# A hybrid decoder layer on one core: three 256-column matmuls per weight tile into one set of PSUM columns

## The chip, the cores and the metric

The kernel runs as one program on one core of a Trainium2 chip. The metric is the device time of one execution in microseconds (us): the kernel before takes 2576.43 us, the median of three runs (2575.58 to 2576.53). A profile of one execution tells what each engine did in it: TensorE (PE in the rows, its weight loads PEld), VectorE (DVE), ScalarE (ACT), GpSimd (POOL) and the queues of DMA (SP issues most of them).

## The reference

One layer of a decoder trunk, 256 tokens of 2048 features, everything float32:

```
h = RMSNorm(x); P = h @ W_in               (mLSTM: 4 heads x 256; dilated attention: 8 heads x 128)
x += concat(mLSTM, dilated attention) @ W_out
x += CrossAttention(RMSNorm(x), RMSNorm(mem))        (4 heads of 512, 256 memory tokens; W_xq, W_xk, W_xv, W_xo)
x += PEER(RMSNorm(x))
out = RMSNorm(x)
```

PEER has 16384 experts of one neuron each: `q = h @ W_pq`, for each of 8 heads the best 16 of 128 keys of both halves, from them the best 16 pairs, a softmax over these, and `sum over experts of gate * gelu(u_e . h) * v_e`. The kernel computes `gelu(u_e . h)` of all 16384 experts, multiplies by a gate that is zero for those not picked, and multiplies by the whole table `v`. So nearly all the work is in matrix products that are streamed once from HBM: tiles of 128 partitions x 2048 float32 (1 MB each).

## The kernel before, in words

Features or experts lie on partitions and the 256 tokens in the free dimension. Each operand of a large product is split into two parts of type `float32r`, hi and lo, whose sum is the float32 value. ScalarE casts a half of a weight tile (128 x 1024) to hi (line 111), and VectorE or GpSimd subtracts to get lo (line 112). GpSimd does it in part of the first stage and for the experts' tiles while VectorE picks the experts. The moving operand (the activations) lies in a buffer of 16 chunks of 512 columns: columns 0 to 255 the hi part of 256 tokens, columns 256 to 511 their lo part.

A product keeps three of the four partial products: hi x hi, hi x lo and lo x hi. For a tile of weights `lin_a` goes over 16 chunks of the contraction. For each it issues two matmuls: hi weights times 512 columns (line 126), which writes hi x hi to PSUM columns 0 to 255 and hi x lo to columns 256 to 511; and lo weights times the first 256 columns (line 127), which adds to columns 256 to 511. The experts' second table has the same pair of matmuls in `v_tile` (lines 818 and 819), the gates of the mLSTM heads in lines 242 and 243. After the last chunk the two halves of the PSUM tile are added: ScalarE copies one half out, VectorE adds the other (`join` at line 253, `join_scaled` at 523, `residual_block` at 185 to 188, `u_block` at 629 and 630, the queries of the experts at 691 and 692), or VectorE adds both to the residual (lines 823 and 824). The other kind of product, `lin_b` (lines 138 to 140), has the activations as weights and 512 columns of weights as the moving operand; it issues three matmuls of 512 columns into the same PSUM columns.

Every matmul has a weight load of its own in the trace (13610 of each), also where it has the same weights as the one before it, as in lines 138 and 139.

The program runs in this order. From 0 to about 330 us the projections of both groups of heads, with the small work of the heads in generators that go one step on after each tile of weights. From about 330 us to 870 us `W_out`, the keys, queries and values of the cross attention, and `W_xo`. From 870 us to 1070 us the product with `W_pq` and the picking of experts, mostly on VectorE, with some blocks of the table `u` (`u_block`) between. From 1070 us to 1290 us the remaining blocks of the first 32, and between them the gates, which are spread into a dense table by one-hot products (`gate_group`, lines 748, 749 and 755). From 1290 us to 2540 us the table `v` (128 tiles, `v_tile`) with the remaining 96 blocks of `u` between. A scheduler puts the instructions of each engine in order when the program is built; on the chip each engine goes through its own in that order, and waits for the others by semaphores. The loads of weights have three buffers (line 97), hi and lo three each.

Of the kernel before, what the change touches and what calls it, by code (L numbers as in the profile page):

```python
# [10 lines left out]
F32 = mybir.dt.float32  # L11
# [9 lines left out]
P = 128  # L21
# [27 lines left out]
def hybrid_layer(ctx: ExitStack, tc: tile.TileContext, a, out):  # L49
# [53 lines left out]
    def wsplit(st, lo_engine=None, order=(0, 1)):  # L103
        """the parts of the tile's two halves; lo_engine "both" gives the half used last to GpSimd"""
# [16 lines left out]

    def lin_a(ps, hi, lo, mov, kcs=range(KC)):
        """ps[:, :256] + ps[:, 256:] = W.T @ h; mov(k) holds both parts of h's chunk."""
        kcs = list(kcs)
        for n, k in enumerate(kcs):
            PE.matmul(ps, hi(k * P), mov(k), start=(n == 0), stop=False)  # L126
            PE.matmul(ps[:, 256:], lo(k * P), mov(k)[:, :256], start=False,  # L127
                      stop=(n == len(kcs) - 1))

    def lin_b(pss2, kg, hi, lo, h):  # L130
        """pss2[tt] += h[:, tt].T @ W for four chunks of the contraction."""
# [10 lines left out]
    def rstd_of(dst, ss, n):  # L142
        """dst = (ss / n + eps) ** -0.5: a first guess from the exponent's bits, three steps of Newton's method"""
# [28 lines left out]
    def as_column(row, name):  # L172
        """[P, 256] with equal partitions -> [P, 2], tokens on partitions."""
# [8 lines left out]
    def residual_block(pool, ps, n, g_at, acc, nxt, first):  # L182
        """resid += ps; acc += resid ** 2; nxt = both parts of resid * g"""
        tmp = pool.tile([P, T], F32, tag="rtmp", name=f"rtmp{n_mm[0]}", bufs=2)
        S.copy(tmp, ps[:, 256:])
        x = resid[:, n, :]
        V.tensor_tensor(x, x, ps[:, :256], op=OP.add)
        V.tensor_tensor(x, x, tmp, op=OP.add)
# [32 lines left out]
    with tc.tile_pool(name="ph1", bufs=2) as p1:  # L221
# [9 lines left out]
        hm = lambda k: h[:, k, :]  # noqa: E731  # L231
        ps_g = mm_tile()
        parts = []
        for i in range(4):
# [5 lines left out]
            for k in range(4 * i, 4 * i + 4):  # L240
                c = (k - 4 * i) * P
                PE.matmul(ps_g, hi[:, c:c + P], hm(k), start=(k == 0), stop=False)
                PE.matmul(ps_g[:, 256:], lo[:, c:c + P], hm(k)[:, :256], start=False, stop=(k == KC - 1))
# [5 lines left out]
        def join(dst, ps, tag):  # L249
            """dst = ps[:, :256] + ps[:, 256:]"""  # L250
            tmp = p1.tile([P, T], F32, tag="jtmp", name=f"jtmp{n_mm[0]}_{tag}")
            S.copy(tmp, ps[:, 256:])
            V.tensor_tensor(dst, ps[:, :256], tmp, op=OP.add)

        def head_norm(sq_parts, n, name):
            """rstd over the head's features, on every partition"""
# [9 lines left out]
        def proj_rows(src, dst):  # L266
            """one group of 512 columns, tokens on partitions: dst [P, 2, 512]"""
# [15 lines left out]
        def start_chain():  # L283
# [8 lines left out]
            for dst, r0, b_at in ((gi, 0, S_BI), (gf, 32, S_BF)):  # L292
                S.copy(gt, ps_g[r0:r0 + 4, 256:])
                S.copy(gu, ps_g[r0:r0 + 4, :256])
                V.tensor_tensor(dst, gu, gt, op=OP.add)
# [85 lines left out]
        rows, ogs = {}, {}  # L381

        def mlstm_in(hd):
            """causal conv on the head's two blocks of channels"""
# [4 lines left out]
            for j in range(2):  # L389
                blk = 2 * hd + j  # L390
                ps = mm_tile()
# [3 lines left out]
                join(xin[:, 3:], ps, f"in{blk}")  # L395
                V.tensor_tensor(xin[:, 3:], xin[:, 3:], rx, op=OP.mult)
# [9 lines left out]
        def mlstm_chain(hd, c32, wq):  # L406
# [4 lines left out]
            # decay weights exp(a_s - max_t), keys on partitions  # L411
# [10 lines left out]
            # q, k: [features, tokens]  # L422
# [23 lines left out]
            # denominator, on every partition  # L446
# [29 lines left out]
        def output_gate(hd):  # L476
            og = p1.tile([P, 2, T], F32, tag="og", name=f"og_{hd}")
            for j in range(2):
                ps = mm_tile()
                lin_a(ps, *wtile(a["w_mo"][2 * hd + j], "both"), hm)  # L480
                join(og[:, j, :], ps, f"o{hd}{j}")
                V.tensor_tensor(og[:, j, :], og[:, j, :], stat["row"], op=OP.mult)
# [15 lines left out]
    # ================= cross attention =================  # L498
    with tc.tile_pool(name="ph2", bufs=1) as p2:
# [18 lines left out]
        mm_ = lambda k: mh[:, k, :]  # noqa: E731  # L518

        def join_scaled(dst, ps, r):  # L520
            tmp = p2.tile([P, T], F32, tag="jt", name=f"jt{n_mm[0]}", bufs=2)
            S.copy(tmp, ps[:, 256:])
            V.tensor_tensor(dst, ps[:, :256], tmp, op=OP.add)
            if r is not None:
                V.tensor_tensor(dst, dst, r, op=OP.mult)
# [435 lines left out]
```

## Time and profile before

| | |
|---|---|
| median of three runs | 2576.43 us |
| span of the profiled execution, first to last instruction | 2554.4 us |
| what lies around the span (median less span) | 22.0 us |
| TensorE busy | 2436.9 us, 95% of the span, 13610 matmuls and as many weight loads |
| VectorE busy | 1724.6 us, 68% |
| ScalarE busy | 1202.1 us, 47% |
| GpSimd busy | 401.6 us, 16% |
| DMA | 466.78 MB, 183 GB/s |

A page of the profile gives the busy time of each engine and its share of the span. TensorE's matmuls are pipelined and their ends are modelled, so rows of neighbouring matmuls overlap, and the pace is read from the distance between two starts. A row "x2048 | 734.2, 400" is a group of 2048 instructions with 734.2 us of busy time and 400 ns mean duration. Where a timeline row has "x2", it merges two neighbours of one line. The profiled execution's time outside its span is not in the profile; the three runs lie within 1 us of each other, so the table takes the difference to their median.

### The profile page before, as it was taken

Reading aid. Unit: us, or ns where it says so; the run is one execution under the profiler, and the core shown is the slowest. Engines: PE = TensorE matmul, PEld = TensorE weight load, DVE = VectorE, ACT = ScalarE, POOL = GpSimd, SP = SyncE. Lnnn points to the kernel's source line nnn. Section 1 sums busy time; section 2 is a strip of 40 time slices with the busy share of each in tenths; the row PEclk is TensorE's granted clock in tenths of the full one; section 3 lists DMA queues with packets and bytes.
Section 4 is the critical chain, followed back from the end, with each engine's and each line's share of the span. In section 5 each row is a group of like instructions: output and inputs, shape, how many; then the busy total and the mean of one; then the engine's idle time right before and its main releaser. Section 6 shows DMA issues by size and latency. Waiting matters only on the chain.

```text
span 2554.4 us, 34778 instructions
## 1 busy us (share of the span) xinstructions
PE 2436.9 (95%) x13610; PEld 2117.2 (83%) x13610; DVE 1724.6 (68%) x2818; ACT 1202.1 (47%) x1649; POOL 401.6 (16%) x214
## 2 busy tenths in 40 slices
PE   7989999999999879788899999999999999999997
PEld 6777788888888768677888888888888888888886
DVE  6877758744456699899975555655655655556565
ACT  6555446444445434355554444444444444444343
POOL 3131313100001457545400000000000000000001
PEclk9999999999999989899999999999999999999998
DMA  6344435544544434344485656555655565555553
GB/s 244 140 144 148 139 125 205 191 168 173 175 176 169 166 119 162 128 167 184 183 289 213 211 188 208 204 194 202 209 203 184 212 212 200 197 184 183 196 198 116
DMA packets 98710, 466.78 MB, mean 183 GB/s; under 512 B 7537, under 2 KB 41585, under 8 KB 45297
## 3 DMA queue, kind: packets, MB, share of 16 engines
q1 hardware_dynamic: 96096, 447.71, 49.4%
q10 hardware_dynamic: 2448, 16.85, 1.6%
q8 instruction: 107, 1.75, 0.3%
q14 instruction: 59, 0.48, 0.1%
HBM read 445.65 MB, written 18.87 MB: 182 GB/s over the span
## 4 chain that ended last, share of the span: by engine, by line
PE 50%; DVE 14%; issue 1%; POOL 0%; DMA 0%; ACT 0%; DVEq 0%; POOLq 0%; SPq 0%; ACTq 0%
PE sm L818 16%; PE mm L126 15%; PE sm L819 8%; PE mm L127 8%; DVE ob L748 4%; DVE oa L749 4%; PE mm L818 2%; PE mm L819 1%; DVE cand L677 1%; DVE xs L645 0%; POOL wlo L112 0%; DVE hsc L163 0%; DVE eq L711 0%; DVE ut L630 0%; DVE eq L709 0%
## 5 line engine op out<-in xcount | busy, mean ns | idle before, releaser
L112 DVE TENSOR_TENSOR wlo<-wst,whi 128x1024 fp32r<-128x1024 f32 x672 | 825.5, 1230 | 692.0 <-ACT whi L111 689.3
L111 ACT CAST whi<-wst 128x1024 fp32r<-128x1024 f32 x800 | 834.2, 1049 | 937.5 <-PE mm L126 531.0
L126 PE MATMUL mm<-hsc,whi 128*128 128x512 f32 x2048 | 734.2, 400 | 4.1 <-ACT whi L111 4.1
L818 PE MATMUL sm<-coef,whi 128*128 128x512 f32 x1792 | 624.7, 391 | 0.0
L127 PE MATMUL mm<-hsc,wlo 128*128 128x256 f32 x2048 | 581.4, 284 | 9.9 <-POOL wlo L112 8.4
L819 PE MATMUL sm<-coef,wlo 128*128 128x256 f32 x1792 | 500.6, 280 | 0.0
L126 PEld LDWEIGHTS mm<-hsc,whi 128*128 128x128 f32 x2048 | 391.5, 191 | 91.5 <-ACT whi L111 5.0
L127 PEld LDWEIGHTS mm<-hsc,wlo 128*128 128x128 f32 x2048 | 395.1, 193 | 12.2 <-POOL wlo L112 10.3
L818 PEld LDWEIGHTS sm<-coef,whi 128*128 128x128 f32 x1792 | 335.2, 187 | 74.0
L112 POOL TENSOR_TENSOR wlo<-wst,whi 128x1024 fp32r<-128x1024 f32 x128 | 315.6, 2473 | 403.0 <-ACT whi L111 382.3
L819 PEld LDWEIGHTS sm<-coef,wlo 128*128 128x128 f32 x1792 | 338.3, 189 | 0.1
L198 POOL TENSOR_TENSOR facc<-facc,rsqf 128x256 f32<-128x256 f32 x11 | 11.9, 1084 | 1224.2 <-ACT rsqf L197 1224.0
L126 PE MATMUL mm<-h,whi 128*128 128x512 f32 x512 | 187.0, 407 | 0.0
L631 ACT ACTIVATE act<-ut 128x256 f32<-128x256 f32 x128 | 53.6, 419 | 216.3 <-DVE ut L630 216.3
L127 PE MATMUL mm<-h,wlo 128*128 128x256 f32 x512 | 145.4, 284 | 4.3 <-DVE wlo L112 4.0
L748 DVE TENSOR_SCALAR ob<-con,selT 128x128 f32<-128x128 f32 x256 | 127.1, 496 | 6.8 <-PE sm L727 6.8
L749 DVE TENSOR_SCALAR oa<-con,selT 128x128 f32<-128x128 f32 x256 | 119.4, 466 | 0.0
L126 PEld LDWEIGHTS mm<-h,whi 128*128 128x128 f32 x512 | 97.8, 191 | 22.8 <-issue 0.3
L198 POOL TENSOR_TENSOR acc<-acc,rsqr 128x256 f32<-128x256 f32 x30 | 39.2, 1308 | 430.1 <-ACT rsqr L197 425.5
L127 PEld LDWEIGHTS mm<-h,wlo 128*128 128x128 f32 x512 | 98.4, 192 | 6.8 <-DVE wlo L112 5.3
L126 PE MATMUL mm<-hp,whi 128*128 128x512 f32 x256 | 97.6, 420 | 3.3 <-DVE hp L158 3.3
L126 PE MATMUL mm<-ocat,whi 128*128 128x512 f32 x256 | 90.5, 399 | 0.0
(309 smaller groups left out, 3375.6 us busy)
## 6 DMA issues: line engine op xcount, KB each, us to landing
wst<-in_uT SPq DMA_DIRECT2D x128, 1024.0 KB, 4.8
wst<-in_v SPq DMA_DIRECT2D x128, 1024.0 KB, 4.8
wst<-in_w_aqk SPq DMA_DIRECT2D x16, 1024.0 KB, 4.8
wst<-in_w_out SPq DMA_DIRECT2D x16, 1024.0 KB, 4.8
wst<-in_w_xk SPq DMA_DIRECT2D x16, 1024.0 KB, 4.8
wst<-in_w_xq SPq DMA_DIRECT2D x16, 1024.0 KB, 4.8
wst<-in_w_xv SPq DMA_DIRECT2D x16, 1024.0 KB, 4.8
wst<-in_w_xo SPq DMA_DIRECT2D x16, 1024.0 KB, 4.8
```

What stands on the lines that cost most here:

```text
L111: S.copy(hi, src)
L112: eng.tensor_tensor(lo, src, hi.bitcast(F32), op=OP.subtract)
L126: PE.matmul(ps, hi(k * P), mov(k), start=(n == 0), stop=False)
L127: PE.matmul(ps[:, 256:], lo(k * P), mov(k)[:, :256], start=False, stop=(n == len(kcs) - 1))
L198: G.tensor_tensor(acc, acc, sq, op=OP.add)
L631: S.activation(act[:, b % RING, :], tmp, AF.Gelu)
L677: V.tensor_tensor(cand, ts[:, tt, hd, 0, :, None].to_broadcast([P, TK, TK]), ts[:, tt, hd, 1, None, :].to_broadcast([P, TK, TK]), op=OP.add)
L748: V.tensor_scalar(ob[:, i, :], iota, selT[:, 1, t:t + 1], None, op0=OP.is_equal)
L749: V.tensor_scalar(oa[:, i, :], iota, selT[:, 0, t:t + 1], selT[:, 2, t:t + 1], op0=OP.is_equal, op1=OP.mult)
L818: PE.matmul(ps, hi(at), coef[:, c, :], start=(c == 0), stop=False)
L819: PE.matmul(ps[:, 256:], lo(at), coef[:, c, :256], start=False, stop=(c == EB - 1))
```

## The change

Each chunk of these products is now three matmuls of 256 columns into the same 256 columns of PSUM: hi weights times the hi columns, hi weights times the lo columns, lo weights times the hi columns. The sum of the halves is thus made in PSUM, and what added them later goes. The three products that were in columns 0 to 255 and 256 to 511 are the same three. `lin_b` isn't changed. Comments are gone as well; the lines of the changed kernel have other numbers.

```
+    def three(ps, hi, lo, mov, first, last):
+        PE.matmul(ps, hi, mov[:, :T], start=first, stop=False)
+        PE.matmul(ps, hi, mov[:, T:], start=False, stop=False)
+        PE.matmul(ps, lo, mov[:, :T], start=False, stop=last)
...
     def lin_a(ps, hi, lo, mov, kcs=range(KC)):
         kcs = list(kcs)
         for n, k in enumerate(kcs):
-            PE.matmul(ps, hi(k * P), mov(k), start=(n == 0), stop=False)
-            PE.matmul(ps[:, 256:], lo(k * P), mov(k)[:, :256], start=False,
-                      stop=(n == len(kcs) - 1))
+            three(ps, hi(k * P), lo(k * P), mov(k), n == 0, n == len(kcs) - 1)
...
     def residual_block(pool, ps, n, g_at, acc, nxt, first):
-        tmp = pool.tile([P, T], F32, tag="rtmp", name=f"rtmp{n_mm[0]}", bufs=2)
-        S.copy(tmp, ps[:, 256:])
         x = resid[:, n, :]
-        V.tensor_tensor(x, x, ps[:, :256], op=OP.add)
-        V.tensor_tensor(x, x, tmp, op=OP.add)
+        V.tensor_tensor(x, x, ps, op=OP.add)
...
                     lin_a(ps, *wtile(a["w_aqk"][2 * hd + w], "both"), hm)
-                    join(qs[:, w, :], ps, f"a{hd}{w}")
+                    S.copy(qs[:, w, :], ps)
...
-                join(xin[:, 3:], ps, f"in{blk}")
-                V.tensor_tensor(xin[:, 3:], xin[:, 3:], rx, op=OP.mult)
+                V.tensor_tensor(xin[:, 3:], ps, rx, op=OP.mult)
...
         def u_block(b, eng=None):
-            ps = mm_tile()
+            ps = mm_tile()[:, :T]
             lin_a(ps, *wtile(a["uT"][b], eng), lambda k: hs[:, k, :])
-            tmp = p3.tile([P, T], F32, tag="ut", name=f"ut{b}")
-            S.copy(tmp, ps[:, 256:])
-            V.tensor_tensor(tmp, ps[:, :256], tmp, op=OP.add)
-            S.activation(act[:, b % RING, :], tmp, AF.Gelu)
+            S.activation(act[:, b % RING, :], ps, AF.Gelu)
...
-                    S.copy(tmp, ps[:, 256:])
-                    V.tensor_tensor(q, ps[:, :256], tmp, op=OP.add)
+                    S.copy(q, ps)
                     chains.append(pick_chain(hd, pp, q, keys))
...
-                    PE.matmul(ps, hi(at), coef[:, c, :], start=(c == 0), stop=False)
-                    PE.matmul(ps[:, 256:], lo(at), coef[:, c, :256], start=False, stop=(c == EB - 1))
+                    three(ps, hi(at), lo(at), coef[:, c, :], c == 0, c == EB - 1)
...
-                        V.tensor_tensor(x, x, accs[j][:, :256], op=OP.add)
-                        V.tensor_tensor(x, x, accs[j][:, 256:], op=OP.add)
+                        V.tensor_tensor(x, x, accs[j], op=OP.add)
```

The keys and queries of the cross attention, the output gates and the mLSTM gates are changed alike: one operation on the 256 columns stands where the copy and the sum stood.

On TensorE, in the middle of the table `v` (second half of weight tile 304; `sm481` to `sm484` are the four PSUM tiles that are summed, `whi304_1` and `wlo304_1` the hi and lo weights, `coef` the moving operand), there stood before:

```order
L818 MATMUL sm481_16802<-coef_11018,whi304_1_16886 128x512
L819 MATMUL sm481_16802<-coef_11018,wlo304_1_16887 128x256
L818 MATMUL sm482_16803<-coef_11018,whi304_1_16886 128x512
L819 MATMUL sm482_16803<-coef_11018,wlo304_1_16887 128x256
L818 MATMUL sm483_16804<-coef_11018,whi304_1_16886 128x512
L819 MATMUL sm483_16804<-coef_11018,wlo304_1_16887 128x256
```

and in the changed kernel, at the same place, there stand:

```order
L124 MATMUL sm481_20466<-coef_12950,whi304_1_20582 128x256
L125 MATMUL sm481_20466<-coef_12950,whi304_1_20582 128x256
L126 MATMUL sm481_20466<-coef_12950,wlo304_1_20583 128x256
L124 MATMUL sm482_20467<-coef_12950,whi304_1_20582 128x256
L125 MATMUL sm482_20467<-coef_12950,whi304_1_20582 128x256
L126 MATMUL sm482_20467<-coef_12950,wlo304_1_20583 128x256
L124 MATMUL sm483_20468<-coef_12950,whi304_1_20582 128x256
L125 MATMUL sm483_20468<-coef_12950,whi304_1_20582 128x256
L126 MATMUL sm483_20468<-coef_12950,wlo304_1_20583 128x256
```

Two matmuls per chunk have become three, with the same sequence of PSUM tiles; over the whole program TensorE's list goes from 12793 to 18697 rows, 5904 more.

On VectorE, at the end of the picking of experts, where the one-hot rows of the gates begin (`eq` and `sel` belong to the picking, `ut` to a block of the table `u`, `ob` and `oa` to the gates), there stood before:

```order
L709 TENSOR_TENSOR eq112_8777<-pf11_8766,con_74 128x512
L711 TENSOR_TENSOR eq112_8777<-eq112_8777,tif_7183 128x512
L630 TENSOR_TENSOR ut7_8881<-mm267_8838,ut7_8881 128x256
L713 TENSOR_REDUCE sel_7186<-eq112_8777 128x32
L709 TENSOR_TENSOR eq113_8781<-pf11_8766,con_74 128x512
L711 TENSOR_TENSOR eq113_8781<-eq113_8781,tif_7183 128x512
L713 TENSOR_REDUCE sel_7186<-eq113_8781 128x32
L630 TENSOR_TENSOR ut8_8928<-mm268_8885,ut8_8928 128x256
L748 TENSOR_SCALAR ob0_9037<-con_74,selT_7177 128x128
L749 TENSOR_SCALAR oa0_9036<-con_74,selT_7177 128x128
```

and in the changed kernel:

```order
L687 TENSOR_TENSOR eq112_10371<-pf11_10360,con_74 128x512
L689 TENSOR_TENSOR eq112_10371<-eq112_10371,tif_8475 128x512
L691 TENSOR_REDUCE sel_8478<-eq112_10371 128x32
L687 TENSOR_TENSOR eq113_10375<-pf11_10360,con_74 128x512
L689 TENSOR_TENSOR eq113_10375<-eq113_10375,tif_8475 128x512
L691 TENSOR_REDUCE sel_8478<-eq113_10375 128x32
L726 TENSOR_SCALAR ob0_10696<-con_74,selT_8469 128x128
L727 TENSOR_SCALAR oa0_10695<-con_74,selT_8469 128x128
```

The additions of `ut` are gone from VectorE's list; the rest stands in the order it had.

## Rows read from the trace of the kernel before

**Rows 1.** The page: the span, busy time and share of each engine, and TensorE's busy tenths in 40 slices of the span.

```profile
span 2554.4 us, 34778 instructions
PE 2436.9 (95%) x13610; PEld 2117.2 (83%) x13610; DVE 1724.6 (68%) x2818; ACT 1202.1 (47%) x1649; POOL 401.6 (16%) x214
PE   7989999999999879788899999999999999999997
```

**Rows 2.** The chain that ended last, as shares of the span by engine.

```profile
PE 50%; DVE 14%; issue 1%; POOL 0%; DMA 0%; ACT 0%; DVEq 0%; POOLq 0%; SPq 0%; ACTq 0%
```

**Rows 3.** Busy time in five stretches of the span. Columns: from:to, length, busy us of PE, PEld, DVE, ACT and POOL with the number of instructions, granted TensorE clock (1.00 is full), DMA share, GB/s.

```profile
0.00:330.00 330.00, 295.37 (x1469) 244.83 (x1470) 241.90 (x412) 176.28 (x288) 88.34 (x54) 0.97 0.45 160
330.00:870.00 540.00, 534.06 (x2873) 458.43 (x2871) 329.93 (x445) 265.76 (x401) 72.18 (x54) 1.00 0.49 176
870.00:1070.00 200.00, 163.66 (x864) 140.26 (x865) 186.40 (x539) 74.50 (x108) 121.93 (x50) 0.90 0.38 133
1070.00:1290.00 220.00, 196.07 (x1210) 175.60 (x1209) 216.17 (x537) 117.53 (x151) 104.58 (x44) 0.94 0.48 181
1290.00:2540.00 1250.00, 1247.79 (x7200) 1098.07 (x7199) 739.65 (x865) 567.98 (x703) 11.92 (x11) 1.00 0.57 201
```

**Rows 4.** The chunks in each stretch: the same five stretches for line 126 alone (the hi matmul of `lin_a`; the first bracket is its count), then the last stretch for line 818 alone (that of `v_tile`), then the group of line 242 over the whole span.

```profile
0.00:330.00 330.00, 164.23 (x448) 85.82 (x448) 0.97 0.45 160
330.00:870.00 540.00, 387.53 (x1103) 206.82 (x1103) 1.00 0.49 176
870.00:1070.00 200.00, 152.20 (x397) 80.46 (x397) 0.90 0.38 133
1070.00:1290.00 220.00, 138.16 (x357) 72.51 (x356) 0.94 0.48 181
1290.00:2540.00 1250.00, 536.17 (x1536) 287.26 (x1536) 1.00 0.57 201
...
1290.00:2540.00 1250.00, 713.27 (x2048) 383.19 (x2048) 1.00 0.57 201
...
L242 PE MATMUL mm<-h,whi_f 128*128 128x512 f32 x16 | 7.9, 506 | 8.2 <-DVE h L158 7.6 <-ACT whi_f L162 0.6
```

**Rows 5.** The timeline of TensorE in a tile of `lin_b`, 512 columns in every matmul: start us, duration us, and the instruction. The first and the last of 23 rows in a row without a wait.

```profile
106.66 0.40 PE L139 MATMUL mm<-wlo,h 128*128 128x512 f32 x1
...
111.65 0.40 PE L140 MATMUL mm<-whi,h 128*128 128x512 f32 x1
```

**Rows 6.** The timeline of TensorE in `lin_a` of the cross attention's queries: the first two rows of a run of 56 pairs of matmuls without a wait, the third row, and the row that begins the pair after the last.

```profile
720.51 0.39 PE L126 MATMUL mm<-hc,whi 128*128 128x512 f32 x1
720.74 0.27 PE L127 MATMUL mm<-hc,wlo 128*128 128x256 f32 x1
720.86 0.40 PE L126 MATMUL mm<-hc,whi 128*128 128x512 f32 x1
...
739.92 0.39 PE L126 MATMUL mm<-hc,whi 128*128 128x512 f32 x1
```

**Rows 7.** Two places in `W_out` where the scheduler put two 256-column matmuls in a row (x2 merges them), with the rows that follow.

```profile
394.40 0.39 PE L127 MATMUL mm<-cat,wlo 128*128 128x256 f32 x2
394.63 0.40 PE L126 MATMUL mm<-cat,whi 128*128 128x512 f32 x1
...
406.54 0.40 PE L127 MATMUL mm<-cat,wlo 128*128 128x256 f32 x2
406.78 0.40 PE L126 MATMUL mm<-cat,whi 128*128 128x512 f32 x1
```

**Rows 8.** The timeline of the table `v` around 2000 us, weight loads (PEld) and matmuls (PE): start us, duration us.

```profile
1999.89 0.28 PE L819 MATMUL sm<-coef,wlo 128*128 128x256 f32 x1
1999.89 0.19 PEld L818 LDWEIGHTS sm<-coef,whi 128*128 128x128 f32 x1
2000.01 0.39 PE L818 MATMUL sm<-coef,whi 128*128 128x512 f32 x1
2000.01 0.19 PEld L819 LDWEIGHTS sm<-coef,wlo 128*128 128x128 f32 x1
```

**Rows 9.** Groups on VectorE (busy us, mean ns of one): the two one-hot operations and the additions of `u_block` from 1070 to 1290 us, then the additions for the experts' queries and those of `u_block` from 870 to 1070 us.

```profile
L748 DVE TENSOR_SCALAR ob<-con,selT 128x128 f32<-128x128 f32 x256 | 127.1, 496 | 6.8 <-PE sm L727 6.8
L749 DVE TENSOR_SCALAR oa<-con,selT 128x128 f32<-128x128 f32 x256 | 119.4, 466 | 0.0
L630 DVE TENSOR_TENSOR ut<-mm,ut 128x256 f32<-128x256 f32 x22 | 9.0, 410 | 0.0
...
L692 DVE TENSOR_TENSOR pq<-mm,pqt 128x256 f32<-128x256 f32 x16 | 6.6, 410 | 3.1 <-ACT pqt L691 3.1
L630 DVE TENSOR_TENSOR ut<-mm,ut 128x256 f32<-128x256 f32 x9 | 3.7, 411 | 0.0
```

**Rows 10.** The first 330 us: two groups of joins on VectorE, and the longest wait of TensorE (us in total, times, longest).

```profile
L253 DVE TENSOR_TENSOR qs<-mm,jtmp_a 128x256 f32<-128x256 f32 x16 | 6.6, 414 | 0.0
L253 DVE TENSOR_TENSOR xin<-mm,jtmp_in 128x256 f32<-128x256 f32 x8 | 3.3, 417 | 0.0
...
PE sm L330 <- DVE qs L326: 10.1, 5, 2.7
```

**Rows 11.** The end of the table `v`: the second addition of the last PSUM tile on VectorE, start and duration.

```profile
2537.33 0.42 DVE L824 TENSOR_TENSOR resid<-resid,mm 128x256 f32<-128x256 f32 x1
```

More of the change, by code (lines that the diff above doesn't have):

```diff
@@ L231, in hybrid_layer @@
         hm = lambda k: h[:, k, :]
-        ps_g = mm_tile()
+        ps_g = mm_tile()[:, :T]
         parts = []
@@ L241, in hybrid_layer @@
                 c = (k - 4 * i) * P
-                PE.matmul(ps_g, hi[:, c:c + P], hm(k), start=(k == 0), stop=False)
-                PE.matmul(ps_g[:, 256:], lo[:, c:c + P], hm(k)[:, :256], start=False, stop=(k == KC - 1))
+                three(ps_g, hi[:, c:c + P], lo[:, c:c + P], hm(k), k == 0, k == KC - 1)
         part = p1.tile([P, T], F32, name="sq_x", bufs=1)
@@ L247, in hybrid_layer @@
         cat = big("cat")
-        def join(dst, ps, tag):
-            tmp = p1.tile([P, T], F32, tag="jtmp", name=f"jtmp{n_mm[0]}_{tag}")
-            S.copy(tmp, ps[:, 256:])
-            V.tensor_tensor(dst, ps[:, :256], tmp, op=OP.add)
         def head_norm(sq_parts, n, name):
@@ L292, in start_chain @@
             for dst, r0, b_at in ((gi, 0, S_BI), (gf, 32, S_BF)):
-                S.copy(gt, ps_g[r0:r0 + 4, 256:])
-                S.copy(gu, ps_g[r0:r0 + 4, :256])
-                V.tensor_tensor(dst, gu, gt, op=OP.add)
+                S.copy(dst, ps_g[r0:r0 + 4, :])
                 V.tensor_tensor(dst, dst, rx[:4, :], op=OP.mult)
@@ L390, in mlstm_in @@
                 blk = 2 * hd + j
-                ps = mm_tile()
+                ps = mm_tile()[:, :T]
                 lin_a(ps, *wtile(a["w_min"][blk], "both"), hm)
@@ L478, in output_gate @@
             for j in range(2):
-                ps = mm_tile()
+                ps = mm_tile()[:, :T]
                 lin_a(ps, *wtile(a["w_mo"][2 * hd + j], "both"), hm)
-                join(og[:, j, :], ps, f"o{hd}{j}")
-                V.tensor_tensor(og[:, j, :], og[:, j, :], stat["row"], op=OP.mult)
+                V.tensor_tensor(og[:, j, :], ps, stat["row"], op=OP.mult)
                 if j == 1:
@@ L518, in hybrid_layer @@
         mm_ = lambda k: mh[:, k, :]
-        def join_scaled(dst, ps, r):
-            tmp = p2.tile([P, T], F32, tag="jt", name=f"jt{n_mm[0]}", bufs=2)
-            S.copy(tmp, ps[:, 256:])
-            V.tensor_tensor(dst, ps[:, :256], tmp, op=OP.add)
-            if r is not None:
-                V.tensor_tensor(dst, dst, r, op=OP.mult)
         hc = big("hc")
@@ L530, in hybrid_layer @@
         for n in range(KC):
-            ps = mm_tile()
+            ps = mm_tile()[:, :T]
             lin_a(ps, *wtile(a["w_out"][n], None, (1, 0)), cm, list(range(8, KC)) + list(range(8)))
@@ L539, in memory_keys @@
             for i in range(4):
-                ps = mm_tile()
+                ps = mm_tile()[:, :T]
                 lin_a(ps, *wtile(a["w_xk"][4 * hd + i]), mm_)
-                join_scaled(kmT[:, i, :], ps, s_mem["row"])
+                V.tensor_tensor(kmT[:, i, :], ps, s_mem["row"], op=OP.mult)
                 tick()
@@ L590, in hybrid_layer @@
             for i in range(4):
-                ps = mm_tile()
+                ps = mm_tile()[:, :T]
                 lin_a(ps, *wtile(a["w_xq"][4 * hd + i]), xm)
-                join_scaled(q[:, i, :], ps, None)
+                S.copy(q[:, i, :], ps)
                 tick()
@@ L611, in hybrid_layer @@
         for n in range(KC):
-            ps = mm_tile()
+            ps = mm_tile()[:, :T]
             lin_a(ps, *wtile(a["w_xo"][n]), om)
@@ L625, in u_block @@
         def u_block(b, eng=None):
-            ps = mm_tile()
+            ps = mm_tile()[:, :T]
             lin_a(ps, *wtile(a["uT"][b], eng), lambda k: hs[:, k, :])
-            tmp = p3.tile([P, T], F32, tag="ut", name=f"ut{b}")
-            S.copy(tmp, ps[:, 256:])
-            V.tensor_tensor(tmp, ps[:, :256], tmp, op=OP.add)
-            S.activation(act[:, b % RING, :], tmp, AF.Gelu)
+            S.activation(act[:, b % RING, :], ps, AF.Gelu)
         selT = p3.tile([P, 3, T], F32, name="selT", bufs=1)
@@ L686, in hybrid_layer @@
                     n = 2 * hd + pp
-                    ps = mm_tile()
+                    ps = mm_tile()[:, :T]
                     lin_a(ps, *wtile(a["w_pq"][n], G), hpm)
                     q = pg.tile([P, T], F32, tag="pq", name=f"pq{n}")
-                    tmp = pg.tile([P, T], F32, tag="pqt", name=f"pqt{n}")
-                    S.copy(tmp, ps[:, 256:])
-                    V.tensor_tensor(q, ps[:, :256], tmp, op=OP.add)
+                    S.copy(q, ps)
                     chains.append(pick_chain(hd, pp, q, keys))
@@ L809, in v_tile @@
                     for j in range(4):
-                        accs[j] = new()
+                        accs[j] = new()[:, :T]
                 order = [(b, j) for b in range(4) for j in range(4)]
```

## The prediction

> **What bounds the kernel now.** I read the page first: TensorE is busy for 95% of the span, the next engine for 68% [rows 1], and half of the chain that ended last is TensorE's, most of the rest VectorE's [rows 2]. An average over a program of such different parts settles little, so I read the busy time by stretch [rows 3]. From 1290 to 2540 us TensorE is busy for 1247.8 of 1250 us at the full granted clock (1.00, the 2.4 GHz level): whatever TensorE gains or loses there shows in full. From 330 to 870 us it is 534 of 540, nearly the same. From 1070 to 1290 us VectorE has 216 of 220 us and TensorE 196: VectorE bounds. From 870 to 1070 us VectorE has 186 of 200 and TensorE 164. In the first 330 us no engine is full: TensorE 295, VectorE 242; TensorE's longest wait there is 10.1 us in five pieces for the scores of a head [rows 10].
>
> So the question is first what three matmuls of 256 columns cost TensorE against one of 512 and one of 256. The number of columns is the same, 768. What can differ is a cost per matmul.
>
> **The price of a matmul, from starts.** A busy TensorE is no measure here, since durations overlap; the pace is the distance of starts. Where all matmuls have 512 columns, 22 of them take 111.65 - 106.66 = 4.99 us, or 226.8 ns each [rows 5]. In the pairs of 512 and 256 columns, 56 pairs take 739.92 - 720.51 = 19.41 us, or 346.6 ns a pair [rows 6]. The 256-column matmul of a pair therefore costs 346.6 - 226.8 = 119.8 ns, more than half of 226.8 (113.4). Split into a part per column and a part per matmul: 256 columns are 226.8 - 119.8 = 107.0 ns, and 119.8 - 107.0 = 12.8 ns is left for each matmul, whatever its width. (107.0 ns for 256 columns is 2.39 columns per ns, the granted full level.) Three matmuls of 256 columns are 3 x 119.8 = 359.4 ns a chunk in place of 346.6: 12.8 ns, or 3.7%, more.
>
> The bounds of this price. Single starts inside a pair are no reading of it: the 256-column matmul starts 0.23 us after the 512-column one, and the next 0.12 us later [rows 6], which would make 512 columns dearer here than in rows 5; the stamps of the two kinds seem shifted by some 3 ns, and only sums over whole pairs count. Two 256-column matmuls in a row occur in the trace where the scheduler had put them so: from the first of them to the next hi matmul it takes 394.63 - 394.40 = 0.23 us in one place and 406.78 - 406.54 = 0.24 us in the other [rows 7], so 115 to 120 ns each. At 115 ns a chunk is 345 ns, 1.6 ns less than now; at 120 ns it is 360. I take 119.8, which comes from sums over 22 and 112 matmuls, and keep 115 as the low end.
>
> Does the third weight load fit? Each matmul brings a load. Before, the load of the hi weights starts with the 256-column matmul ahead of it (both at 1999.89), and its own matmul starts at 2000.01 [rows 8]: 0.12 us of a 256-column matmul are enough to hide a load. In the changed kernel each load has such a matmul ahead of it, and no more is asked. If a load could not be hidden so, its price is the recorded 0.19 us [rows 8]; three of them would be 0.57 us a chunk.
>
> Rows 5 and 6 give 226.8 ns for 512 columns, of which 12.8 belong to no column. The Trainium skill, "TensorE: Matmul & The Clock Gate" (section "Wait — 56ns, not 53.3ns?"), has a fixed cost of only about 2.5 ns per warm matmul on top of the columns at 2.4 GHz, 215.8 ns for 512 columns; the trace differs, and decides. An estimate by that rule of the page would be 2.5 ns more a chunk.
>
> **The change stretch by stretch.** The chunks are counted by the hi matmul of each [rows 4]: 448 + 16 in the first 330 us, 1103 from 330 to 870, 397 + 357 from 870 to 1290, and 1536 + 2048 = 3584 in the last. At 12.8 ns each:
>
> From 1290 to 2540 us: 3584 x 12.8 = 45.9 us, all on the path, since TensorE has no idle time to put it in [rows 3]. What is removed here (the copy on ScalarE and the addition on VectorE per block of `u`, one of two additions per tile of sums) is on engines that are busy for 568 and 740 of 1250 us, and so is worth nothing. VectorE's lo and ScalarE's hi of the weights are ready ahead already.
>
> From 330 to 870 us: 1103 x 12.8 = 14.1 us. There are 6 us of idle time of TensorE in 540, but these are waits for things that TensorE itself delays; I count all 14.1.
>
> From 870 to 1290 us: 754 x 12.8 = 9.7 us more for TensorE, beside VectorE, which loses 22 additions of 410 ns (9.0 us) after 1070 us and 25 before (16 for the queries, 9 for blocks of `u`: 10.3 us) [rows 9]. After 1070 us VectorE is full and its list is otherwise the same, so the whole 9.0 us comes off; TensorE has 24 us free there and takes 357 x 12.8 = 4.6 us more beside it. Before 1070 us parts of the chain are TensorE's and GpSimd's, and VectorE has gaps; of the 10.3 us less the 5.1 us that TensorE gains I count 4 as a saving. Together -13. The ends are -19.3 (all additions on the path, TensorE beside them) and +9.7 (TensorE alone on the path).
>
> From 0 to 330 us: 464 x 12.8 = 5.9 us for TensorE, which is busy for 295 of 330 us. VectorE loses 24 joins, 6.6 + 3.3 = 9.9 us [rows 10], some of which stand ahead of the scores that TensorE waits for. The ends are -9.9 and +5.9. I take +2: most of the tiles of this stretch run at TensorE's pace, and the wait that a shorter chain could take away is 10.1 us in all [rows 10].
>
> At the end one addition of 0.42 us after the last matmul of `v` goes [rows 11]: -0.4.
>
> The sum: 45.9 + 14.1 - 13 + 2 - 0.4 = +48.6 us. Against the profiled execution: 2554.4 + 48.6 = 2603.0 us of span. What lies around the span is 22.0 us to the median of the runs, and nothing in the change touches it: 2625 us, 1.9% slower.
>
> **The rivals.**
>
> *A 256-column matmul behind another costs only 115 to 116 ns, and the kernel gets faster.* The mechanism would be that the dear one in a pair is the 512-column matmul that is followed by a 256-column one. Place: the 3584 + 1103 chunks of the full stretches. For it: the 0.23 us for two [rows 7]. Against it: 512 columns cost 226.8 ns in rows 5, and a pair of these with 115 to 116 would take 342 to 343 ns, not 346.6. Price at 115 ns: 4687 x -1.6 = -7.5 us, and the smaller stretches with no load on TensorE give -13 - 1 - 0.4; together -22, 2554 us. It decides for faster as soon as three matmuls cost less than 346.6 + 11.4 / 4.687 = 349.0 ns, 116.3 each (11.4 us being the savings elsewhere: 13 + 0.4 - 2).
>
> *The cost per matmul is there, but small.* At the middle of rows 7, 117.5 ns, a chunk is 352.5 ns: 4687 x 5.9 = 27.7 us, less 11.4: 2593 us. At 116.3 ns, where savings and cost cancel, it would be no change, 2576 us; it needs both stretches of rows 5 and 6 to mislead, so I give that little. The page's 2.5 ns leads, as an estimate, to about the same end: 4687 x 2.5 = 11.7 us against savings of 11.4.
>
> *VectorE's savings don't arrive.* If from 870 to 1290 us TensorE or the GpSimd subtractions take over as the bound, all 5905 chunks cost 12.8 ns: 75.6 us, 2652 us. For it: GpSimd has 122 of 200 us in the stretch before 1070 us [rows 3] and holds up TensorE at places. Against it: VectorE at 216 of 220.
>
> *The load of the same weights a second time isn't hidden.* Three loads at 0.19 us each are 0.57 us a chunk, 0.22 us more: 4687 x 0.22 = about 1030 us, 3600 us. Against it are rows 8 and rows 5, where two thirds of the matmuls that follow one another in `lin_b` load other weights and the rest the same ones again, all at 226.8 ns on average. I leave it out of the range. That the change doesn't do what it says is ruled out by TensorE's list: 5904 more matmuls.
>
> **How the numbers follow.** The forecast, 2610 to 2640 us (its own range, from the ends of the two stretches that VectorE shares), 0.58. Savings don't arrive, 2640 to 2656: 0.14. Small cost, 2582 to 2610: 0.14. No change, at a price near 116.3 ns: 0.05. Faster: 0.06. Load not hidden or something else far above: 0.03. The range that should hold the time 8 times in 10 leaves out the 0.11 of faster and no change, the lowest part of the small cost and the highest of the rest: 2590 to 2653. 0.2% of 2576 is 5.2 us, about what a measurement of this kernel can tell from no change. Faster by more: 0.06; within: 0.05; slower by more: 0.89.
>
> **What would show it.** In the table `v` of the changed kernel, the start of every third matmul 359 ns after that of three before (345 would be the first rival, 352 the small cost), and 128 tiles of `v` with 96 blocks of `u` in about 1296 us in place of 1250. From 1070 to 1290 us VectorE still full and the stretch 9 us shorter; if TensorE is full there instead, the savings didn't arrive. Pairs of starts at 0.57 us would be the load. A granted clock below 1.00 in the last stretch, or idle time of TensorE there, would mean that I have misread what bounds it.

## The result and the profile after

The changed kernel takes 2587.17 us, the median of ten runs (2585.35 to 2589.04); the kernel before, in ten runs, 2575.94 us (2558.85 to 2584.49). The ratio is 1.0056, with a 95% interval of 1.0036 to 1.0075: slower, but by 11 us where 49 were forecast, and outside the range of 2590 to 2653. Note the spread of the ten runs: 3.7 us after, 25.6 us before.

The page of the changed kernel, the parts that answer to [rows 1, 2]:

```profile
span 2584.1 us, 45917 instructions
PE 2496.8 (97%) x19514; PEld 2436.2 (94%) x19514; DVE 1610.2 (62%) x2448; ACT 1139.5 (44%) x1453; POOL 396.2 (15%) x214
...
PE 77%; DVE 19%; ACT 2%; issue 1%; DMA 1%; POOL 1%; DVEq 0%; SPq 0%; ACTq 0%; POOLq 0%
```

5904 matmuls more, VectorE 114 us and ScalarE 63 us less busy. This profiled execution took 2585.87 us for a span of 2584.1: only 1.8 us lie around a span. Busy time in the same stretches as [rows 3]:

```profile
0.00:330.00 330.00, 304.88 (x1969) 277.73 (x1970) 235.40 (x385) 174.73 (x278) 88.72 (x55) 0.98 0.46 163
330.00:870.00 540.00, 535.30 (x3926) 511.09 (x3925) 304.63 (x374) 245.79 (x342) 67.77 (x51) 1.00 0.49 173
870.00:1070.00 200.00, 168.94 (x1307) 166.59 (x1306) 190.89 (x526) 74.56 (x103) 128.35 (x54) 0.91 0.41 146
1070.00:1290.00 220.00, 208.75 (x1672) 202.88 (x1672) 210.99 (x510) 117.87 (x137) 99.71 (x41) 0.98 0.52 192
1290.00:2540.00 1250.00, 1250.00 (x10419) 1250.00 (x10418) 645.35 (x619) 514.49 (x576) 5.71 (x7) 1.00 0.56 196
```

The last stretch is full, as before. From 1070 to 1290 us TensorE rises from 196 to 209 us and its granted clock from 0.94 to 0.98; VectorE has a little room for the first time. The timeline of TensorE, the answer to [rows 6]: three matmuls of 256 columns per chunk, one start every 0.12 us (10557 of the 10569 distances of starts in the last stage are 120 ns).

```profile
1905.88 0.28 PE L125 MATMUL mm<-hsc,whi 128*128 128x256 f32 x1
1906.00 0.28 PE L126 MATMUL mm<-hsc,wlo 128*128 128x256 f32 x1
1906.12 0.28 PE L124 MATMUL mm<-hsc,whi 128*128 128x256 f32 x1
1906.24 0.28 PE L125 MATMUL mm<-hsc,whi 128*128 128x256 f32 x1
```

The program falls into four stages, which can be told apart by the first matmul of `W_out`, of `W_pq` and of the table `v`. Lengths in us, from the timelines of the profiled executions; the last runs to the end of the span:

| execution | to `W_out` | to `W_pq` | to `v` | to the end | span |
|---|---|---|---|---|---|
| before, as shown ahead of the prediction | 380.3 | 482.2 | 453.8 | 1238.1 | 2554.4 |
| before, another execution (below) | 383.3 | 481.0 | 453.2 | 1261.4 | 2578.9 |
| changed kernel | 373.0 | 493.4 | 432.8 | 1284.9 | 2584.1 |
| three matmuls, joins kept | 386.5 | 491.0 | 446.6 | 1286.8 | 2610.9 |
| pair, no joins | 371.4 | 481.3 | 432.6 | 1263.5 | 2548.8 |
| join on VectorE alone | 371.8 | 480.6 | 468.9 | 1258.3 | 2579.6 |
| three matmuls, copy on VectorE | 370.4 | 492.8 | 442.5 | 1286.7 | 2592.4 |
| hi, lo, hi | 367.7 | 494.3 | 437.5 | 1285.7 | 2585.1 |
| before, regrouped | 377.2 | 481.1 | 449.6 | 1248.0 | 2555.9 |
| three where there is slack | 372.6 | 480.8 | 439.0 | 1241.4 | 2533.8 |
| the same, regrouped | 374.2 | 479.3 | 435.6 | 1248.1 | 2537.2 |

Against the execution that the prediction was made from, the changed kernel's span is 29.7 us longer: -7.3, +11.2, -21.0 and +46.8. The two long stages came out as forecast (14.1 and 45.9); the two others gave back more. Each row is one profile: the two of the kernel before differ by up to 3.0 us in their first three stages, and "hi, lo, hi", which only changes the order of the three matmuls, by 5.3 and 4.7 us from the changed kernel in the first and the third. A few us in these two stages are no effect.

### The profile page after: what moved, and what is told of

It is laid out like the page before. It is cut to its first block, busy times and chain, and to the rows that moved or that the text cites. A ratio compares the mean times of both kernels' runs of the same rounds, so it can differ in the third digit from the quotient of the medians.

```text
span 2584.1 us, 45917 instructions
## 1 busy us (share of the span) xinstructions
PE 2496.8 (97%) x19514; PEld 2436.2 (94%) x19514; DVE 1610.2 (62%) x2448; ACT 1139.5 (44%) x1453; POOL 396.2 (15%) x214
## 4 chain that ended last, share of the span: by engine, by line
PE 77%; DVE 19%; ACT 2%; issue 1%; DMA 1%; POOL 1%; DVEq 0%; SPq 0%; ACTq 0%; POOLq 0%
PE mm L124 14%; PE mm L125 14%; PE mm L126 14%; PE sm L125 8%; PE sm L124 8%; PE sm L126 8%; DVE oa L727 4%; DVE ob L726 3%; PE mm L143 2%; PE mm L144 2%; PE mm L142 2%; DVE wlo L112 1%; DVE eq L689 1%; DVE eq L687 1%; DVE nt L155 1%
## 5 line engine op out<-in xcount | busy, mean ns | idle before, releaser
L124 PE MATMUL mm<-hsc,whi 128*128 128x256 f32 x2048 | 586.3, 286 | 1.4 <-ACT whi L111 1.4
L125 PE MATMUL mm<-hsc,whi 128*128 128x256 f32 x2048 | 583.5, 285 | 0.0
L124 PE MATMUL sm<-coef,whi 128*128 128x256 f32 x1792 | 507.1, 283 | 0.0
L125 PE MATMUL sm<-coef,whi 128*128 128x256 f32 x1792 | 507.1, 283 | 0.0
L126 PE MATMUL sm<-coef,wlo 128*128 128x256 f32 x1792 | 507.1, 283 | 0.0
L124 PEld LDWEIGHTS mm<-hsc,whi 128*128 128x128 f32 x2048 | 397.4, 194 | 1.9 <-ACT whi L111 1.9
L125 PEld LDWEIGHTS mm<-hsc,whi 128*128 128x128 f32 x2048 | 397.4, 194 | 0.0
L124 PEld LDWEIGHTS sm<-coef,whi 128*128 128x128 f32 x1792 | 344.1, 192 | 0.0
L125 PEld LDWEIGHTS sm<-coef,whi 128*128 128x128 f32 x1792 | 344.1, 192 | 0.0
L126 PEld LDWEIGHTS sm<-coef,wlo 128*128 128x128 f32 x1792 | 344.1, 192 | 0.0
L124 PE MATMUL mm<-h,whi 128*128 128x256 f32 x512 | 149.1, 291 | 0.0
L125 PE MATMUL mm<-h,whi 128*128 128x256 f32 x512 | 146.3, 286 | 0.0
L727 DVE TENSOR_SCALAR oa<-con,selT 128x128 f32<-128x128 f32 x256 | 132.8, 519 | 0.0
L726 DVE TENSOR_SCALAR ob<-con,selT 128x128 f32<-128x128 f32 x256 | 112.2, 438 | 0.8 <-PE sm L705 0.8
```

What stands on the lines that cost most here:

```text
L124: PE.matmul(ps, hi, mov[:, :T], start=first, stop=False)
L125: PE.matmul(ps, hi, mov[:, T:], start=False, stop=False)
L126: PE.matmul(ps, lo, mov[:, :T], start=False, stop=last)
L726: V.tensor_scalar(ob[:, i, :], iota, selT[:, 1, t:t + 1], None, op0=OP.is_equal)
L727: V.tensor_scalar(oa[:, i, :], iota, selT[:, 0, t:t + 1], selT[:, 2, t:t + 1], op0=OP.is_equal, op1=OP.mult)
```

## The experiments

**The kernel before, again.** No edit. The kernel before had runs 26 us apart, and its profile's span was shorter than the fastest of them by 4.5 us, more than the 1.8 us that lie around a span.

> The kernel before, unchanged, to see how its executions differ from each other and where. Theory A (an execution varies in the stretches that VectorE bounds or shares, since TensorE's clock drops there when it waits): span between 2555 and 2582 us, the granted clock lower in the longer ones, the stretch from 1290 to 2540 us within 1 us of 1250. Theory B (the full stretches vary): that stretch itself differs by 10 us or more.

Measured: 2579.26 us, median of 12 runs from 2557.49 to 2582.16. The first three stages are within 3 us of the profile before; the last is 23.3 us longer. Theory B holds. In the stretch from 1290 to 2540 us the engine isn't waiting, the clock is full, and yet fewer matmuls go through (7076; [rows 3] have 7200):

```profile
1290.00:2540.00 1250.00, 1248.11 (x7076) 1082.51 (x7076) 730.88 (x853) 560.21 (x692) 9.78 (x10) 1.00 0.57 200
```

The timeline of TensorE there, first and last of 17 pairs:

```profile
1799.74 0.40 PE L126 MATMUL mm<-hsc,whi 128*128 128x512 f32 x1
1799.98 0.28 PE L127 MATMUL mm<-hsc,wlo 128*128 128x256 f32 x1
1800.11 0.40 PE L126 MATMUL mm<-hsc,whi 128*128 128x512 f32 x1
...
1805.75 0.40 PE L818 MATMUL sm<-coef,whi 128*128 128x512 f32 x1
```

17 pairs in 6.01 us are 353.5 ns a pair; [rows 6] had 346.6. So the pair of 512 and 256 columns has two paces, 346.7 and 353.3 ns in the means over the table `v`, and the 3525 chunks of the last stage x 6.7 ns = 24 us are the difference between the two profiles.

Both paces stand in the first profile too, outside the table `v`. In `W_xo`, 40 us after the run of [rows 6], 15 pairs take 785.10 - 779.80 = 5.30 us, 353.3 ns each:

```profile
779.80 0.40 PE L126 MATMUL mm<-ocat,whi 128*128 128x512 f32 x1
...
785.10 0.40 PE L126 MATMUL mm<-ocat,whi 128*128 128x512 f32 x1
```

The mean over the uninterrupted pairs from 330 to 870 us is 349.5 ns there. A pace belongs to a series of alternating pairs that no wait and no change of order interrupts. In the five profiles with alternating pairs (two of the kernel before, "pair, no joins", "three where there is slack", "join on VectorE alone") there are 305 such series of 13 pairs or more, and 293 keep one pace from the fifth pair to the last. The table `v` is one series of about 3000 pairs, then a place where the scheduler put two 512-column matmuls together and soon after two of 256, then a series of 502 pairs. In the profile of "three where there is slack" the pace goes from 346.7 to 353.3 ns just there:

```profile
2336.98 0.39 PE L826 MATMUL sm<-coef,whi 128*128 128x512 f32 x1
2337.21 0.28 PE L827 MATMUL sm<-coef,wlo 128*128 128x256 f32 x1
2337.33 0.63 PE L826 MATMUL sm<-coef,whi 128*128 128x512 f32 x2
2337.80 0.28 PE L827 MATMUL sm<-coef,wlo 128*128 128x256 f32 x1
2337.92 0.39 PE L826 MATMUL sm<-coef,whi 128*128 128x512 f32 x1
2338.15 0.40 PE L827 MATMUL sm<-coef,wlo 128*128 128x256 f32 x2
2338.39 0.40 PE L826 MATMUL sm<-coef,whi 128*128 128x512 f32 x1
```

In that of "join on VectorE alone" it changes at the same place the other way, at 2386 us; in the two of the kernel before the place is passed without a change. So the pace that the long series takes up at its start is worth 3000 x 6.7 ns = 20 us of an execution. The run times agree: of the 74 runs of the kernel before, 13 took 2557 to 2566 us, 61 took 2572 to 2587, and none lies between.

**Three matmuls, joins kept.** The joins of the kernel before come back, with a maximum of the sum and its own copy in place of the addition of halves, and two additions per sum of `v`:

```
+            tmp = p3.tile([P, T], F32, tag="ut", name=f"ut{b}")
+            S.copy(tmp, ps)
+            V.tensor_tensor(tmp, ps, tmp, op=OP.max)
-            S.activation(act[:, b % RING, :], ps, AF.Gelu)
+            S.activation(act[:, b % RING, :], tmp, AF.Gelu)
```

> The changed kernel with as many copies and additions after each product as before (a copy on ScalarE, a maximum of the copy and the sum on VectorE, and two additions per tile of the table v), so only the matmuls differ from the kernel before. Theory A (each 256-column matmul costs 120 ns, and the work that was removed gave back some 20 to 40 us in the stretches where TensorE isn't full): 2610 to 2630 us, in the table v 46 us more than before. Rival B (the removed work was worth little, and the matmuls cost only 11 us): 2585 to 2592 us.

Measured: 2609.76 us, ratio 1.0115 (1.0099 to 1.0131). Theory A, 0.2 us below its range: with three matmuls the joins are worth 23 us. They show in the first stage (+13.5 us against the changed kernel) and the third (+13.8); the others differ by -2.4 and +1.9. In the last stage it is 48.7 us over the profile before and 25.4 over the other execution: "46 us more than before" was right only for the faster pace.

**The pair, no joins.** The other half of the change:

```
-        PE.matmul(ps, hi, mov[:, :T], start=first, stop=False)
-        PE.matmul(ps, hi, mov[:, T:], start=False, stop=False)
-        PE.matmul(ps, lo, mov[:, :T], start=False, stop=last)
+        PE.matmul(ps, hi, mov, start=first, stop=False)
+        PE.matmul(ps[:, :T], lo, mov[:, :T], start=False, stop=last)
```

> The pair of matmuls of 512 and 256 columns of before, with the lo product added to the first 256 columns and the evacuation of the changed kernel, which reads these alone: the product of hi weights and lo activations is left out of the result. Theory A: 20 to 40 us under the kernel before, 2535 to 2556 us, all of it before 1290 us. Rival B: within 8 us of the kernel before.

Measured: 2537.4 us (2523.43 to 2552.41), ratio 0.9828 (0.9790 to 0.9865). In the first and third stages it gains 8.9 and 21.2 us against the profile before, as much as the changed kernel (7.3 and 21.0): there TensorE's additional matmuls cost next to nothing, and the gain comes without them. At the same pace the last stage gains nothing (1263.5 us against 1261.4), as theory A had it. With three matmuls the joins were worth 13.5 and 13.8 us in the first and third stages, not 8.9 and 21.2. Part of this is the scatter of a stage; and the third stage with three matmuls and all joins is 7 us shorter than that of the kernel before, which no run explains. The granted clock from 1070 to 1290 us rose with the gain (0.94 before, 0.98 in the changed kernel, 0.97 here), and its part is not separated. The six runs lie in two groups, 2523 to 2526 and 2548 to 2552 us, 25 us apart: here the table `v` is a single series of 3510 pairs in the profile, and 3510 x 6.7 ns = 23 us. The median lies between the groups, where no run does.

**What a join costs.** Two runs ask whether it is VectorE's time or the way over ScalarE (its copy, and the hand-over from it to VectorE). First, the kernel before with both steps on VectorE:

```
-            S.copy(tmp, ps[:, 256:])
+            V.tensor_copy(tmp, ps[:, 256:])
             V.tensor_tensor(dst, ps[:, :256], tmp, op=OP.add)
```

> The kernel before with both steps of the join on VectorE (a copy of one half, then the addition) in the first stretch, for the experts' queries and for the blocks of u, so nothing waits for ScalarE in between and VectorE has more work. Theory E (before 380 us the join costs by its hand-over from ScalarE to VectorE, from 865 to 1317 us half by that and half by VectorE's time): the first stretch 8 to 12 us shorter than before, the stretch of the picking and the gates 0 to 10 us longer. Rival F (only the amount of work counts): the first stretch no shorter than before, the other 10 us or more longer, 2585 us or more in all.

Measured: 2582.1 us, ratio 1.0012 (0.9989 to 1.0036). The first stage is 8.5 us shorter than in the profile before and 11.5 shorter than in the other execution, with more work on VectorE: there VectorE's time was not the cost, and theory E's number came true. That it is the hand-over is argued and not shown, since the run also takes the copy off ScalarE. The third is 15.1 us longer, for 51 copies of 0.41 us, 21 us: there VectorE's time counts for some 70%, theory E's 0 to 10 us was wrong, and rival F's 10 or more held. Second, the changed kernel with its copies on VectorE:

```
-                    S.copy(q, ps)
+                    V.tensor_copy(q, ps)
```

> The changed kernel with the evacuation of each product by a copy on VectorE in place of ScalarE (queries and keys of both attentions, inputs and gates of the mLSTM heads, queries of the experts, blocks of u). Theory A (what the removed joins gave back was VectorE's time before 330 us and from 870 to 1290 us): 2604 to 2618 us, the loss in these two stretches and none in the table v. Rival (it was the shorter chain from product to use, or ScalarE's time): within 8 us of the changed kernel.

Measured: 2594.88 us, ratio 1.0075 (1.0049 to 1.0100), 7.7 us over the changed kernel: at the edge of the rival's bound, far under theory A's. In the first stage this agrees with the run before: nothing is lost (2.6 us shorter). The third is 9.7 us longer, about half the time of its 51 copies; with the scatter of 5 us the two runs bound VectorE's share there only roughly.

**Three where there is slack.** Three matmuls and no joins in the first stage, for the experts' queries and for the first 32 blocks of `u`; the pair elsewhere.

```
+            if eng is G:
+                ps = mm_tile()[:, :T]
+                lin_3(ps, *wtile(a["uT"][b], eng), lambda k: hs[:, k, :])
+                S.activation(act[:, b % RING, :], ps, AF.Gelu)
+                return
```

> Three matmuls and no join in the first stretch, for the experts' queries and for the first 32 blocks of u; the pair and the join elsewhere (330 to 870 us and after 1290 us). Theory A: both gains, 2525 to 2556 us. Rival B: between the two kernels, 2575 to 2588 us.

Measured: 2551.96 us, ratio 0.9888 (0.9867 to 0.9910). Theory A. Its runs go from 2535.63 to 2557.82 us; the pair with its two paces is still there from 330 to 870 us and in the table `v`.

**The same pairs, regrouped.** If alternation makes the second pace, runs of equal matmuls should not have it:

```
+        for at in range(0, len(kcs), 8):
+            for n in range(at, at + 8):
+                PE.matmul(ps, hi(kcs[n] * P), mov(kcs[n]), start=(n == 0), stop=False)
+            for n in range(at, at + 8):
+                PE.matmul(ps[:, 256:], lo(kcs[n] * P), mov(kcs[n])[:, :256], start=False,
+                          stop=(n == len(kcs) - 1))
```

> The kernel before with the same regrouping of its pairs and nothing else. Theory C: 2552 to 2562 us in every run, the table v in 1220 us, mean distance of starts 226.7 and 120.0 ns. Rival D: a median near 2578 us with single runs down to 2557, as the kernel before.

> As the run with three matmuls only where TensorE has slack, and the pairs of the other stretches regrouped: eight hi matmuls of 512 columns in a row, then their eight lo matmuls of 256 (four and four in the last quarter of a group of sums). Theory C (the pace of a pair, 346.7 or 353.3 ns, comes from the alternation of the two widths; among equals a matmul has 226.7 or 120.0 ns and nothing else): always the fast pace, 2530 to 2540 us in every run, spread under 8 us. Rival D (the pace is a state of the chip or of the execution, whatever the order): 2532 to 2558 us, spread as before.

Measured: the kernel before with this edit alone 2555.74 us (six runs from 2554.54 to 2557.8), ratio 0.9919 (0.9890 to 0.9948); with three matmuls where there is slack 2538.46 us (2537.33 to 2540.78), ratio 0.9854 (0.9825 to 0.9883), the fastest median that computes the whole result. The spread is that of theory C, and so are the times, but for two of the six runs of the second, up to 0.8 us over 2540. The pace is not quite: the timeline of the first shows eight pairs from one hi group to the next.

```profile
1900.80 2.00 PE L820 MATMUL sm<-coef,whi 128*128 128x512 f32 x8
1902.64 1.11 PE L823 MATMUL sm<-coef,wlo 128*128 128x256 f32 x8
1903.59 2.00 PE L820 MATMUL sm<-coef,whi 128*128 128x512 f32 x8
```

2.79 us for eight pairs are 348.8 ns a pair, between the two paces: a change of width seems to cost something, and eight to a group leave a little of it. All but one of the 373 groups of eight in the last stage take 2793 or 2794 ns, 349.2 ns a pair, so the steady time is no average of two paces. The last stage is 1248.0 us, 10 over the better pace and 13 under the worse. From the first to the last matmul it is 1232.5 us, where theory C had 1220; the total of 2556 us was also helped by 3 to 6 us in the first stage and 4 in the third, which the expectation didn't have.

**Is the same weight again special?** The changed kernel with lo between the two hi matmuls:

```
         PE.matmul(ps, hi, mov[:, :T], start=first, stop=False)
-        PE.matmul(ps, hi, mov[:, T:], start=False, stop=False)
-        PE.matmul(ps, lo, mov[:, :T], start=False, stop=last)
+        PE.matmul(ps, lo, mov[:, :T], start=False, stop=False)
+        PE.matmul(ps, hi, mov[:, T:], start=False, stop=last)
```

> The changed kernel with the order of its three matmuls changed: hi weights times hi columns, lo weights times hi columns, hi weights times lo columns, so no matmul has the weights of the one before it. Theory A (a matmul costs 120.0 ns by its width alone, whatever its weights): 2584 to 2590 us, 120.0 ns everywhere. Rival (a load of the same weights again is cheaper or dearer than one of others): 2 ns or more from 120.0 for one of the three, 14 us or more in the time.

Measured: 2586.31 us, and nearly all starts from 1290 to 2400 us are 119 to 121 ns apart. No: whether the weights are those loaded before makes no difference.

**How thin the cover of a load is.**

```
-        PE.matmul(ps, lo, mov[:, :T], start=False, stop=last)
+        PE.matmul(ps[:, :P], lo, mov[:, :P], start=False, stop=False)
+        PE.matmul(ps[:, P:], lo, mov[:, P:T], start=False, stop=last)
```

> The changed kernel with its third matmul of 256 columns, that of the lo weights, cut into two of 128: four matmuls a chunk and four loads. Theory A (53.3 ns of columns and 13.3 ns of its own for each): 120 + 120 + 66.7 + 66.7 = 373.3 ns a chunk, 62 us more in the stretches that TensorE bounds, 2645 to 2655 us. Rival (a load needs longer than 67 ns, so that it shows behind 128 columns): over 390 ns a chunk, 2730 us or more.

Measured: 3141.71 us, ratio 1.2181. The rival, by far. Loads and matmuls in its timeline, one chunk:

```profile
1900.01 0.19 PEld L124 LDWEIGHTS mm<-hsc,whi 128*128 128x128 f32 x1
1900.07 0.33 PE L124 MATMUL mm<-hsc,whi 128*128 128x256 f32 x1
1900.12 0.19 PEld L125 LDWEIGHTS mm<-hsc,whi 128*128 128x128 f32 x1
1900.24 0.28 PE L125 MATMUL mm<-hsc,whi 128*128 128x256 f32 x1
1900.24 0.19 PEld L126 LDWEIGHTS mm<-hsc,wlo 128*128 128x128 f32 x1
1900.35 0.23 PE L126 MATMUL mm<-hsc,wlo 128*128 128x128 f32 x1
1900.36 0.19 PEld L127 LDWEIGHTS mm<-hsc,wlo 128*128 128x128 f32 x1
1900.42 0.27 PE L127 MATMUL mm<-hsc,wlo 128*128 128x128 f32 x1
...
1900.47 0.19 PEld L124 LDWEIGHTS mm<-hsc,whi 128*128 128x128 f32 x1
1900.53 0.33 PE L124 MATMUL mm<-hsc,whi 128*128 128x256 f32 x1
```

The loads start every 0.11 to 0.12 us, whatever the width of the matmul they belong to, and a chunk takes 1900.53 - 1900.07 = 0.46 us, four of them; the mean chunk from 1600 to 2400 us is 463.3 ns, or 115.8 ns a load. Two matmuls can start closer than that, 1900.42 - 1900.35 = 0.07 us here, so the pace is that of the loads and no least distance of matmuls. The 256-column matmul at 120 ns stands just above it.

## Why the prediction was right and wrong

*What bounds each stretch*: right. The last stretch is TensorE's before and after, and the gain came from the first and third stages. From 1070 to 1290 us VectorE no longer bounds alone: it has 211 of 220 us, TensorE 209.

*The price of a matmul*: right, 119.8 ns forecast from sums and 120.0 measured; the 0.23 us for two [rows 7] was no reading of it. The price of the pair beside it was read from one series of pairs [rows 6], and that series had the better of two paces. The last stage has 46.8 us more than in the profile before, which held that pace there (45.9 forecast); the second has 11.2 (14.1 forecast), and with its mean of 349.5 ns a pair it would be 1103 x 10.5 = 11.6. The fixed cost of about 2.5 ns per warm matmul that the Trainium skill states ("TensorE: Matmul & The Clock Gate", section "Wait — 56ns, not 53.3ns?") doesn't hold for these matmuls: 120.0 ns for 256 columns are 13.3 ns over 256 / 2.4.

*The base of the forecast*: wrong, and the largest single error, 20.2 of the 37.8 us between the forecast 2625 and the measured 2587.2; the first and the third stage make up most of the rest. The step was "What lies around the span is 22.0 us to the median of the runs, and nothing in the change touches it". 1.8 us lie around a span. The other 20 us were that the profiled execution had the pair's better pace through the table `v`, and the others, judging by their times, mostly the worse one, as the second profile shows it. None of the rivals asked whether the pair's own price holds from one execution to the next. The change touches just that: from 353.3 to 360.0 ns a chunk is 6.7 ns, not 12.8 or 13.3. Of the forecast's +48.6 us, some 24 were in the kernel's ordinary time already. That the profile stood 22 us below three runs that agreed within 1 us was a sign that it was not one of their kind.

*The first stage*: mis-sized. Forecast +2, measured -7.3 against the profile before. I had -9.9 as an end, "24 joins", and took a value near TensorE's side, since the waits for scores were 10.1 us in all [rows 10]. The 8 joins of the output gates were left out of that count, 4 of them before 330 us and 4 up to 385. The waits that a shorter chain could take away were more than the 10.1 us for `qs`: those for the softmax of the same heads (`sc`) come to 4.9. Together they fell from 15.0 to 7.4 us, which is the size of the gain. Before:

```profile
PE sm L348 <- DVE sc L344: 4.9, 4, 1.9
```

and in the changed kernel:

```profile
PE sm L322 <- DVE qs L318: 6.8, 6, 2.2
...
PE sm L340 <- DVE sc L336: 0.6, 1, 0.6
```

Putting both steps on one engine gives the gain as well (371.8 us), so the cost of a join there lies in the way over ScalarE and not in VectorE's time.

*The third stage*: mis-sized. Forecast -13, measured -21.0. I counted 4 of 10.3 us before 1070 us and let TensorE's extra work eat into the rest. It cost nothing that the runs show, and the gain is as large as all the additions; -19.3 had been my own low end. Whether the additions alone made it stays open, since the runs give them between 13.8 and 21.2 us.

*The third load*: right that it is hidden; but the cover is only some 4 ns, 120.0 less 115.8. The Trainium skill, the same page, section "LDWEIGHTS (loading the stationary operand)", has a load's time as its columns over 1.2 per ns, 107 ns for 128. The run with 128-column matmuls agrees in kind, with 115.8 ns measured between loads, and the measurement decides.

With the other execution as the base, and the stages as measured, the sum closes. Against the other execution of the kernel before: 23.5 + 12.4 - 20.4 - 10.3 = +5.2 us of span, 2578.9 to 2584.1. The medians differ by 11.2; that execution took 2580.79 us, the median run of before 2575.94, and the changed kernel's profiled run 1.3 us less than its median.

What stays open: what decides which pace a series of pairs takes at its start, and so whether the slower of the two can be avoided with the pairs as they are. Where the pace changed in the middle of the table is known, at the break in the order; that a break changes it is not shown by a run of its own. That alternation of widths is needed for the worse pace is shown by the regrouped kernels' spread, six runs each within 3.5 us where the alternating ones spread over 22 to 29, and by their groups of constant length; a mechanism was not shown.

## What to carry to other kernels

Before a profile is used as the base of a forecast, its span plus the few microseconds around it should match the median of the runs; where it does not, another execution has to be read too, stretch by stretch, for a pace that differs. A pace that was read from one place of a profile should be read at a second place too. Splitting a matmul costs its fixed part only where TensorE bounds, so the split that saves an evacuation belongs in the stages where another engine bounds. A vector addition that waits for another engine's copy can cost more by that way than by its own time; moving the copy to the engine that waits shows whether that engine's time is the cost.

## What the runs showed of the hardware

The pair of a 512- and a 256-column matmul runs at 346.7 or 353.3 ns with the clock granted in full, and a series of such pairs that no wait or change of order interrupts mostly keeps its pace, for as long as 1240 us. Matmuls of one width had one pace, 120.0 ns for 256 columns and 226.8 for 512 [rows 5]. Weight loads of 128 columns followed one another every 115.8 ns on average where they set the pace, so matmuls of 128 columns with a load each came only 4 ns under the 120.0 of 256 columns, and cutting one matmul in three to halves of 128 columns made the whole kernel 22% slower than before.
